# Attention scores computed twice, keys by queries the second time, in place of transposed probabilities

## The chip, the cores and the metric

The kernel runs on one core of one Trainium2 chip. The metric is the device time of one execution in microseconds (us); of several runs the median counts. The engines of the core are TensorE (PE, with its weight loads shown as PEld), VectorE (DVE), ScalarE (ACT), GpSimd (POOL) and SyncE (SP), which issues the DMAs.

## The reference, cut to what matters

One layer of a hybrid backbone over 2048 latent tokens and 256 context tokens, all in float32. Only the attention is touched by the change:

```python
# 8 query heads share 2 key/value heads (4 to each), head_dim 64
# keys: 256 context + 2048 latent tokens = 2304; queries: 2048 latent tokens
s = jnp.einsum('bqkgd,bnkd->bkgqn', q, keys).astype(jnp.float32) * scale
p = jax.nn.softmax(s, axis=-1)
return jnp.einsum('bkgqn,bnkd->bqkgd', p.astype(vals.dtype), vals)
```

Beside it the layer has a gated linear recurrence (HGRN2) in four heads and two directions, an input projection ahead of both, an output projection behind them, and a SwiGLU feed-forward block.

## The kernel before, in words

The stages follow one another: modulation vectors, input projection (with the normalisation and rotation of queries and keys running beside it, `qk_side`, L426), attention together with the recurrence (L566 to L975), output projection (`project_token`, L1005), feed-forward (L1114 to L1264). Matrix products take float32 values as a high part and a low part in a faster type (fp32r): product = high by high, high by low, low by high.

For scores, high and low are packed along the 128 rows of the contraction. `s_k` holds for each key 64 rows of high parts and 64 of low ones; `s_q` holds for each query its high part twice (rows 0 to 63 and 64 to 127), and also its low part twice. Two products into the same PSUM bank give the score. `qk_side` writes `s_q` with four DMAs per 128 tokens and key/value head (L478 to L481), in rows of 2 KB.

The attention is a loop over 64 items (L900): 2 key/value heads, 16 blocks of 128 queries, 2 pairs of heads. An item (`class Pair`, L788) does for each of its two heads, in three segments of 768 keys:

- `scores` (L798): four products with 128 queries as the stationary operand and 512 or 256 keys moving (L812) into one of two PSUM buffers; DVE takes the extremum of the segment (L815; the queries carry a factor -1/8, so a minimum serves as the maximum); ACT computes the exponential with that extremum as bias and sums its rows on the side (L820). For the last segment the extremum of all three is used (L819), and POOL then multiplies the first two segments by a factor (L823, L827).
- `transposes` (L830): the probabilities have queries in the partitions, but the product with V needs keys there. So 36 blocks of 128x128 are transposed by PE (L835), four to a PSUM bank, and copied back to SBUF by ACT, or for two of nine by DVE (L839, L841).
- `products` (L843): 18 products with V as the stationary operand, 64 columns wide, alternating between the lower and the upper 64 partitions of the output (L848). The profile records each float32 product as two.
- `finish` (L860): two transposes back, division by the row sums on DVE (L865 to L870), a sum of the two halves on POOL (L872), a store.

The order of PE's work is written out by hand (`manual_schedule`, L899): PE runs the attention's instructions in the order of the program text. The order on the other engines comes from the tile framework's planner, and each engine's queue is then first in, first out. While item n's scores are computed, item n-1's transposes stand between the segments, and n-1's products come at its end. `other()` (L887) advances the recurrence by 0.88 of a step after five of the six segments. The recurrence has some 276 steps, each a few products on PE (L624 to L727) with element-wise work on POOL (L618 to L661), DVE (L638, L666, L689, L712) and ACT between; two of its units are in progress at a time, and they share one PSUM buffer (`ps_h`).

Of the kernel before, what the change touches and what calls it, by code (L numbers as in the profile page):

```python
# [16 lines left out]
P = 128  # L17
D = 1024
# [25 lines left out]
N_S, N_T, N_H = 2, 2, 1  # L44
LIVE = 2
EV_DVE = (2, 5)
QI = WOE = "gpsimd"
SLOTS, STEPS = 5, 4.4
# [19 lines left out]
def block_kernel(ctx: ExitStack, tc: tile.TileContext, a: dict, out: bass.AP, dbg=None):  # L68
# [21 lines left out]
    s_q = [dram(f"s_q{j}", [NCH, P, 2, 512]) for j in range(2)]  # L90
# [117 lines left out]
    with ExitStack() as st:  # L208
# [217 lines left out]
        def qk_side(t, c):  # L426
# [39 lines left out]
            if isq:  # L466
# [11 lines left out]
                for dup in range(2):  # L478
                    for hh in range(2):
                        nc.sync.dma_start(s_q[c][lt, dup * 64:(dup + 1) * 64, hh],  # L480
                                          f32v(sk[hh * 64:(hh + 1) * 64, :]))  # L481
# [84 lines left out]
    with ExitStack() as st:  # L566
        kvp = pool(st, "kvp", 1, side="right")
        qpl = pool(st, "qpl", 2, side="right")
        sm = pool(st, "sma", 8, side="right")
        pp = pool(st, "pp", 4, side="right")  # L570
        op = pool(st, "op", 1, side="right")
        tp = pool(st, "tp", 9, side="right")
        ps_t2 = pool(st, "ps_t2", N_T, PSUM, side="right")
        ps_av = pool(st, "ps_av", 1, PSUM, side="right")
        hst = ExitStack()
        ps_s2 = pool(hst, "ps_s2", N_S, PSUM)
# [8 lines left out]
        for lv in range(7):  # L585
            mf = up.tile([P, P], F32, tag="kt", name=f"mf{lv}", bufs=4)
            nc.sync.dma_start(mf, a["k_mask"][:, lv, :])
            nc.vector.tensor_copy(mask[:, lv, :], mf)
        nrot = [0]
# [194 lines left out]
        SEG = [(o, SW) for o in range(0, NTOK, SW)]  # L784
        NSEG = len(SEG)
        NKT = NTOK // P

        class Pair:  # L788


            def __init__(self, item, kv, qs):
                self.item, self.kv, self.qs = item, kv, qs
                self.nm = "_".join(map(str, item))
                self.ls = sm.tile([P, 2, NSEG], F32, tag="ls", name=f"ls{self.nm}", bufs=5)
                self.fac = sm.tile([P, 2, NSEG - 1], F32, tag="fac", name=f"fac{self.nm}", bufs=5)
                self.prs, self.negs, self.pf = [], [], {}

            def scores(self, hh, i):  # L798

                nm = f"{self.nm}_{hh}"
                if i == 0:
                    self.prs.append(pp.tile([P, NTOK], F32, tag="pr", name=f"pr{nm}"))
                    self.negs.append(sm.tile([P, NSEG + 1], F32, tag="neg", name=f"neg{nm}"))
                pr, neg = self.prs[hh], self.negs[hh]
                k0, n = SEG[i]
                s = ps_s2.tile([P, 1024], F32, tag="s", name=f"s{i}_{nm}")
                for o in range(0, n, 512):
                    w = min(512, n - o)  # L810
                    for half in range(2):
                        nc.tensor.matmul(s[:, o:o + w], self.qs[:, hh, self.item[2], half, :],  # L812
                                         self.kv[0][:, k0 + o:k0 + o + w],
                                         start=(half == 0), stop=(half == 1))
                nc.vector.tensor_reduce(neg[:, i:i + 1], s[:, :n], axis=AX.X, op=ALU.min)  # L815
                m = i
                if i == NSEG - 1:
                    m = NSEG
                    nc.vector.tensor_reduce(neg[:, NSEG:], neg[:, :NSEG], axis=AX.X, op=ALU.min)  # L819
                nc.scalar.activation(pr[:, k0:k0 + n], s[:, :n], AF.Exp, bias=neg[:, m:m + 1],  # L820
                                     scale=-1.0, accum_out=self.ls[:, hh, i:i + 1])
                if i == NSEG - 1:
                    nc.scalar.activation(self.fac[:, hh, :], neg[:, :NSEG - 1], AF.Exp,  # L823
                                         bias=neg[:, NSEG:], scale=-1.0)
                    for j in range(NSEG - 1):
                        pj = pr[:, j * SW:(j + 1) * SW]
                        nc.gpsimd.tensor_tensor(pj, pj, self.fac[:, hh, j:j + 1].to_broadcast([P, SW]),  # L827
                                                op=ALU.mult)

            def transposes(self, k2):  # L830

                pt = ps_t2.tile([P, 512], F32, tag="t", name=f"pt{self.nm}_{k2}")
                for i in range(2):
                    for hh in range(2):
                        nc.tensor.transpose(pt[:, (2 * i + hh) * P:(2 * i + hh + 1) * P],  # L835
                                            self.prs[hh][:, (2 * k2 + i) * P:(2 * k2 + i + 1) * P], ident)
                pf = self.pf[k2] = tp.tile([P, 512], F32, tag="pf", name=f"pf{self.nm}_{k2}")
                if k2 in EV_DVE:
                    nc.vector.tensor_copy(pf, pt)  # L839
                else:  # L840
                    nc.scalar.activation(pf, pt, AF.Copy)  # L841

            def products(self):  # L843

                self.av = ps_av.tile([P, 256], F32, tag="av", name=f"av{self.nm}")
                for n, k2 in enumerate(T_ORDER):
# [7 lines left out]
            def finish(self):  # L854
                finish(*self.item, self.ot, self.ls, self.fac)
# [452 lines left out]
```

## Time and profile before

| | us |
|---|---|
| median of 3 runs | 3580.23 (3574.32 to 3586.11) |
| the profiled execution | 3583.7 |
| its span, first to last instruction | 3581.9 |
| PE busy in the span | 3352.1 |
| POOL busy in the span | 1593.0 |

A line of groups reads: source line, engine, operation, tile written <- tiles read, shapes, count | busy us in total, mean ns of one | idle time of the engine just ahead of them, and what ended it. A line of the timeline reads: start us, duration us, engine, line, operation, tiles, count [idle before <- what ended it]. A line of waits reads: who <- for whom: us in total, times, longest. Matmuls are pipelined, so the pace of a run of them is read from their starts and not from the duration of one.

### The profile page before, as it was taken

The numbers are of one execution on the slowest core, as the hardware profiler recorded it, in microseconds if no ns is written. First come the engines' busy times: TensorE is split into PE (matmuls) and PEld (weight loads), VectorE is DVE, ScalarE is ACT, GpSimd is POOL, SyncE is SP. The second block draws the span as 40 slices with busy tenths as digits, with TensorE's granted clock in tenths as the row PEclk, the third lists the DMA queues.
The fourth block names the chain that finished last, engine by engine and source line by source line (L and its number), as shares of the span: only waits on it lengthen the run. The fifth ranks groups of instructions, "written<-read, shape, count | busy, mean of one in ns | idle before, by whom it ended". The sixth has DMA issues, their size and how long they took to land. (4 is left out here: it accounts for less than half of the span.)

```text
span 3581.9 us, 52481 instructions
## 1 busy us (share of the span) xinstructions
PE 3352.1 (94%) x19588; PEld 2793.6 (78%) x19588; DVE 1757.0 (49%) x3078; ACT 1549.5 (43%) x3167; POOL 1593.0 (44%) x1496
## 2 busy tenths in 40 slices
PE   8999999979999899999999988999999799999997
PEld 5999877968777778777777876888787678887876
DVE  6445555066667677666655474222354332222344
ACT  4322222157767567766654133333433233333232
POOL 4322232068768758768742046555201165553010
PEclk9999999989999999999999999999999899999998
DMA  7244655321121121111005432222445322222553
GB/s 231 95 140 123 176 167 167 109 85 32 36 63 34 33 69 44 31 46 40 23 24 162 159 106 74 91 76 83 150 146 171 121 92 89 73 88 85 162 173 104
DMA packets 315696, 355.97 MB, mean 99 GB/s; under 512 B 27088, under 2 KB 245168, under 8 KB 315184
## 3 DMA queue, kind: packets, MB, share of 16 engines
q1 hardware_dynamic: 315440, 352.61, 31.7%
q8 instruction: 154, 2.52, 0.3%
q14 instruction: 102, 0.84, 0.1%
HBM read 251.85 MB, written 100.68 MB: 98 GB/s over the span
## 5 line engine op out<-in xcount | busy, mean ns | idle before, releaser
L827 POOL TENSOR_TENSOR pr<-pr,fac 128x768 f32<-128x768 f32 x256 | 374.4, 1484 | 215.0 <-DMA mf<-in_k_mask_dram 101.5
L815 DVE TENSOR_REDUCE neg<-s 128x1 f32<-128x768 f32 x384 | 365.1, 954 | 199.0 <-PE s L812 198.4
L812 PE MATMUL s<-K,qs 128*128 128x512 f32 (+1 forms) x1536 | 371.5, 364 | 33.7 <-ACT pr L820 31.6
L820 ACT ACTIVATE pr<-s,neg 128x768 f32<-128x768 f32 x384 | 348.5, 908 | 73.6 <-DVE neg L819 38.1
L812 PEld LDWEIGHTS s<-K,qs 128*128 128x128 f32 x1536 | 264.0, 191 | 104.8 <-ACT pr L820 44.9
L835 PE MATMUL pt<-identr,pr 128*128 128x128 f32 x2304 | 319.8, 274 | 7.6 <-DVE oo L870 3.2
L841 ACT ACTIVATE pf<-pt 128x512 f32<-128x512 f32 x448 | 256.7, 601 | 111.4 <-PE pt L835 109.5
L1230 PE MATMUL pd<-dl,hh 128*128 128x512 f32 x704 | 277.8, 395 | 2.7 <-DVE dl L1226 2.7
L1230 PE MATMUL pd<-dh,hl 128*128 128x512 f32 x704 | 277.4, 394 | 0.0
L835 PEld LDWEIGHTS pt<-identr,pr 128*128 128x128 f32 x2304 | 261.3, 141 | 16.6 <-ACT pf L841 7.5
L848 PE MATMUL av<-pf,V 128*64 128x256 f32 x2304 | 268.7, 388 | 1.5 <-DVE pf L839 1.5
L848 PEld LDWEIGHTS av<-pf,V 128*64 128x64 f32 x2304 | 162.4, 139 | 88.3 <-issue 9.7
L1230 PE MATMUL pd<-dh,hh 128*128 128x512 f32 x704 | 181.7, 394 | 17.9 <-DVE yy L1244 14.4
L1245 POOL TENSOR_TENSOR yy<-yy,xf 128x512 f32<-128x512 f32 x24 | 30.6, 1296 | 364.6 <-DVE yy L1244 348.7
L1221 ACT ACTIVATE hh<-hr 128x512 fp32r<-128x512 f32 x88 | 55.4, 630 | 292.2 <-PE pd L1230 289.4
L1222 DVE TENSOR_TENSOR hl<-hr,hh 128x512 fp32r<-128x512 f32 x88 | 61.7, 701 | 231.7 <-ACT hh L1221 229.8
L1230 PEld LDWEIGHTS pd<-dh,hh 128*128 128x128 f32 x704 | 133.6, 190 | 48.8 <-DVE yy L1244 16.2
L635 PE MATMUL pa<-Q,M 128*128 128x128 f32 x896 | 131.4, 291 | 30.7 <-POOL Q L661 16.8
L1230 PEld LDWEIGHTS pd<-dl,hh 128*128 128x128 f32 x704 | 134.3, 191 | 31.7 <-DVE dl L1226 3.6
L1230 PEld LDWEIGHTS pd<-dh,hl 128*128 128x128 f32 x704 | 134.3, 191 | 28.2
L635 PEld LDWEIGHTS pa<-Q,M 128*128 128x128 f32 x896 | 116.4, 195 | 38.7 <-POOL Q L661 20.5
L1161 PE MATMUL pA<-x,A11h 128*128 128x512 f32 x352 | 118.9, 403 | 23.9 <-ACT A11h L1135 23.9
(290 smaller groups left out, 8698.8 us busy)
## 6 DMA issues: line engine op xcount, KB each, us to landing
w<-in_w_gu_dram SPq DMA_DIRECT2D x88, 512.0 KB
wr<-in_w_down_dram SPq DMA_DIRECT2D x88, 512.0 KB
wm<-in_w_mod_dram SPq DMA_DIRECT2D x24, 1024.0 KB
s_hid<-h SPq DMA_DIRECT2D x88, 256.0 KB
hr<-s_hid SPq DMA_DIRECT2D x88, 256.0 KB
s_q<-sq SPq DMA_DIRECT2D x128, 128.0 KB
qs<-s_q SPq DMA_DIRECT2D x32, 512.0 KB
ws<-in_w_in_dram SPq DMA_DIRECT2D x9, 1024.0 KB
```

What stands on the lines that cost most here:

```text
L635: nc.tensor.matmul(pa[:, cs], M[:, cs], strided(Q[:], c * P, [[2 * hs, 64 // hs], [512 + hs, 2], [1, hs]]), start=True, stop=True)
L812: nc.tensor.matmul(s[:, o:o + w], self.qs[:, hh, self.item[2], half, :], self.kv[0][:, k0 + o:k0 + o + w], start=(half == 0), stop=(half = ...
L815: nc.vector.tensor_reduce(neg[:, i:i + 1], s[:, :n], axis=AX.X, op=ALU.min)
L820: nc.scalar.activation(pr[:, k0:k0 + n], s[:, :n], AF.Exp, bias=neg[:, m:m + 1], scale=-1.0, accum_out=self.ls[:, hh, i:i + 1])
L827: nc.gpsimd.tensor_tensor(pj, pj, self.fac[:, hh, j:j + 1].to_broadcast([P, SW]), op=ALU.mult)
L835: nc.tensor.transpose(pt[:, (2 * i + hh) * P:(2 * i + hh + 1) * P], self.prs[hh][:, (2 * k2 + i) * P:(2 * k2 + i + 1) * P], ident)
L841: nc.scalar.activation(pf, pt, AF.Copy)
L848: nc.tensor.matmul(self.av[i * 64:(i + 1) * 64], self.kv[1][:, 2 * k2 + i, :], self.pf[k2][:, i * 256:(i + 1) * 256], start=(n == 0), stop ...
L1161: nc.tensor.matmul(acc, w[wi][:, k, :], x[xi][k], start=(start and k == 0 and i == 0), stop=(stop and k == KH - 1 and i == 2), skip_group_ ...
L1221: nc.scalar.activation(hh, hr, AF.Copy)
L1222: nc.vector.tensor_tensor(hl, hr, f32v(hh), op=ALU.subtract)
L1230: nc.tensor.matmul(acc[j][hf], l[:, j * P:(j + 1) * P], r[:, hf * 512:(hf + 1) * 512], start=(ff == 0 and i == 0), stop=(ff == NFF - 1 and ...
```

## The change

Scores are computed twice. The first time is as before, queries by keys, only to find the maximum of each query over all 2304 keys. The second time it is keys by queries (128 keys stationary, 4 heads x 128 queries = 512 columns moving), so that the result already has keys in the partitions. The maximum is subtracted inside the product: a second copy of the keys' high parts (`K2`) has -1 in rows 0 and 1, zeros up to row 63 and the high parts in rows 64 to 127; the low parts of the queries (`ql`) carry the maxima, split into high and low, in rows 0 and 1. ACT then takes the exponential without a bias, and its output goes into the product with V as it is. Row sums are made by adding the 18 tiles of a unit: 7 of the 18 form a chain on DVE and 11 a chain on POOL (the first tile of a chain needs no add), POOL adds the two chains, and four products with a column of ones sum over the partitions.

The unit of work is now 4 heads x 128 queries, 32 units in all. While unit n goes through its 18 tiles of keys (`exps`), the 12 segments of the first score pass of unit n+1 (`maximum`) stand between them. At the end the maxima of n+1 are transposed into two rows (`maxima_in_rows`), and then come the products of n with V. `other` advances the recurrence by 0.47 of a step 19 times per unit. Queries are stored as high parts twice (`s_qh`) and low parts once (`s_ql`), by six DMAs in rows of 512 bytes instead of four in rows of 2 KB. Cut to its core:

```diff
-N_S, N_T, N_H = 2, 2, 1
+N_H = 1
-EV_DVE = (2, 5)
-SLOTS, STEPS = 5, 4.4
+STEP, STEP0 = 0.47, 0.5
+ADD_DVE = (1, 3)
+AT = {1 + 3 * i // 2: (i,) for i in range(12)}
...
-                for dup in range(2):
-                    for hh in range(2):
-                        nc.sync.dma_start(s_q[c][lt, dup * 64:(dup + 1) * 64, hh],
-                                          f32v(sk[hh * 64:(hh + 1) * 64, :]))
+                parts = f32v(sk).rearrange("p (r a t) -> p r a t", r=2, a=2)
+                for hh in range(2):
+                    rows = slice(hh * 64, (hh + 1) * 64)
+                    for dup in range(2):
+                        nc.sync.dma_start(s_qh[c][lt, dup * 64:(dup + 1) * 64, :, hh], parts[rows, :, 0])
+                    nc.sync.dma_start(s_ql[c][lt, :, :, hh], parts[rows, :, 1])
...
+        ps_s1 = pool(hst, "ps_s1", 2, PSUM)
+        ps_s2 = pool(hst, "ps_s2", 2, PSUM)
...
+        K2 = [kvp.tile([P, SW], F32R, name=f"K2_{j}") for j in range(NKB)]
+        QL = [qpl.tile([P, 512], F32R, name=f"ql{j}", bufs=1) for j in range(2)]
+        for t in K2:
+            nc.vector.tensor_copy(t[:64], zero.to_broadcast([64, SW]))
+            nc.vector.tensor_copy(t[:2], less.to_broadcast([2, SW]))
...
+        class Unit:
+            def __init__(self, n):
...
+                nc.sync.dma_start(f32v(self.qh), s_qh[self.g][self.qt].rearrange("p r h t -> p (r h t)"))
+                nc.sync.dma_start(f32v(self.ql[64:]), s_ql[self.g][self.qt].rearrange("p r h t -> p (r h t)"))
+                nc.sync.dma_start(f32v(self.ql[:2]), zrow)
...
+            def maximum(self, i):
...
+                j, b = divmod(i, 4)
+                s = ps_s1.tile([P, 1024], F32, tag="s", name=f"s{self.n}_{i}")
+                for o in range(0, SW, 512):
+                    w = min(512, SW - o)
+                    for half, (q, k) in enumerate(zip((self.qh, self.ql), self.keys(j))):
+                        nc.tensor.matmul(s[:, o:o + w], q[:, b * P:(b + 1) * P], k[:, o:o + w],
+                                         start=(half == 0), stop=(half == 1))
+                nc.vector.tensor_reduce(self.mx[:, b, j:j + 1], s[:, :SW], axis=AX.X, op=ALU.min)
+                if i == 4 * NSEG - 1:
+                    neg = sm.tile([P, 4], F32, tag="neg", name=f"neg{self.n}")
+                    nc.vector.tensor_reduce(neg, self.mx, axis=AX.X, op=ALU.min)
+                    self.mt = sm.tile([P, 4, 2], F32R, tag="mt", name=f"mt{self.n}")
+                    nc.scalar.activation(self.mt[:, :, 0], neg, AF.Copy)
+                    nc.vector.tensor_tensor(self.mt[:, :, 1], neg, f32v(self.mt[:, :, 0]), op=ALU.subtract)
+
+            def maxima_in_rows(self):
+                pm = ps_h.tile([P, 512], F32R, tag="h", name=f"pm{self.n}")
+                for b in range(4):
+                    nc.tensor.transpose(pm[:2, b * P:(b + 1) * P], self.mt[:, b, :], identr)
+                nc.scalar.activation(self.ql[:2], f32v(pm[:2]), AF.Copy)
+
+            def exps(self, t):
+                j, o = t // TSEG, t % TSEG * P
+                s = ps_s2.tile([P, 512], F32, tag="s2", name=f"z{self.n}_{t}")
+                for half, (q, k) in enumerate(zip((self.qh, self.ql), self.keys(j))):
+                    nc.tensor.matmul(s, k[:, o:o + P], q, start=(half == 0), stop=(half == 1))
+                p = tp.tile([P, 512], F32, tag="pT", name=f"pT{self.n}_{t}")
+                nc.scalar.activation(p, s, AF.Exp, scale=-1.0)
+                self.pT.append(p)
+                a = t % 5 in ADD_DVE
+                eng = nc.vector if a else nc.gpsimd
...
+                    eng.tensor_tensor(x, self.acc[a], p, op=ALU.add)
...
+                if t == NKT - 1:
+                    nc.gpsimd.tensor_tensor(self.acc[0], self.acc[0], self.acc[1], op=ALU.add)
+
+            def products(self, V):
+                self.av = ps_av.tile([P, 512], F32, tag="av", name=f"av{self.n}")
+                for t, p in enumerate(self.pT):
+                    i = t % 2
+                    nc.tensor.matmul(self.av[i * 64:(i + 1) * 64], V[:, t, :], p,
+                                     start=(t < 2), stop=(t >= NKT - 2))
...
+            def sums(self):
+                ps = ps_av.tile([P, 512], F32, tag="av", name=f"sum{self.n}")
+                for b in range(4):
+                    nc.tensor.matmul(ps[:, b:b + 1], self.acc[0][:, b * P:(b + 1) * P], ones,
+                                     start=True, stop=True)
...
+        for n in range(NU):
...
+            for t in range(NKT):
...
+                cur.exps(t)
+                if nxt is not None:
+                    for i in AT.get(t, ()):
+                        nxt.maximum(i)
+                if old is not None:
+                    if t == 2:
+                        old.sums()
+                    if t == 4:
+                        old.finish()
...
+                other(STEP)
+            if n + 2 < NU:
+                units[n + 2] = Unit(n + 2)
+            other(STEP)
+            if nxt is not None:
+                nxt.maxima_in_rows()
...
+            cur.products(V)
```

More of the change, by code (lines that the diff above doesn't have):

```diff
@@ L783, in block_kernel @@
         SW = 768
[L784 to L785 removed]
+        NSEG = NTOK // SW
         NKT = NTOK // P
[L788 to L802, printed above, removed]
[L803 to L855 removed]
@@ L876, in load_kv @@
[L876 to L883 removed]
+        TSEG = SW // P
+        NKB = NSEG + 1
+        zero = op.tile([64, 1], F32, name="zero")
```

220 lines of the change are left out of this document (111 added, 109 removed).

## The prediction

> **What bounds the kernel now.** First the page's busy line and, from the busy times by stretch, the row of the attention stage (columns: PE, PEld, DVE, ACT, POOL busy, clock, DMA share, GB/s).
>
> ```profile
> PE 3352.1 (94%) x19588; PEld 2793.6 (78%) x19588; DVE 1757.0 (49%) x3078; ACT 1549.5 (43%) x3167; POOL 1593.0 (44%) x1496
> 729.40:1911.00 1181.60, 1073.21 (x8072) 892.07 (x8072) 799.86 (x1358) 803.82 (x1827) 851.47 (x907) 0.98 0.16 48
> ```
>
> TensorE (PE) is busy 94% of the span, and 91% of the attention stage, where POOL (72%), ACT and DVE (68% each) are loaded too and DMA (16%) is not. The change lies in this stage, so I read its PE timeline next: its ends, and one item whole.
>
> ```profile
> 729.46 1.65 PE L812 MATMUL s<-K,qs 128*128 128x512 f32 x8
> ...
> 772.79 4.11 PE L848 MATMUL av<-pf,V 128*64 128x256 f32 x36
> ...
> 1003.05 4.11 PE L848 MATMUL av<-pf,V 128*64 128x256 f32 x36
> 1007.09 0.97 PE L812 MATMUL s<-K,qs 128*128 128x512 f32 x4
> 1007.90 1.04 PE L835 MATMUL pt<-identr,pr 128*128 128x128 f32 x8
> 1008.69 0.95 PE L812 MATMUL s<-K,qs 128*128 128x512 f32 x4
> ...
> 1019.71 4.11 PE L848 MATMUL av<-pf,V 128*64 128x256 f32 x36
> ...
> 1882.81 4.11 PE L848 MATMUL av<-pf,V 128*64 128x256 f32 x36
> ...
> 1925.09 4.11 PE L848 MATMUL av<-pf,V 128*64 128x256 f32 x36
> ```
>
> The L848 groups stand at the end of each of the 64 items; two come after 1882.81, so 61 items lie between 772.79 and 1882.81: 18.2 us each, **36.4 us for a pair**, which is one unit of the changed kernel. Within an item PE hardly rests: products 4.04 us (1003.05 to 1007.09), a segment of scores 0.81, eight transposes 0.79. The last L848 ends at 1925.09 + 4.04 = 1929.1, but output-projection products run among the last items:
>
> ```profile
> 1900.00:1924.20 24.20, 14.53 (x57) 10.25 (x57) 0.97 0.43 134
> ```
>
> That row is line L1018 alone; without its 14.5 us the stage ends at 1914.6. **The stage is 1914.6 - 729.5 = 1185 us.** What PE and its weight loads wait for in it:
>
> ```profile
> PE pd L624 <- DVE T L666: 12.9, 1, 12.9
> PEld s L812 <- ACT pr L820: 44.9, 51, 8.1
> PEld pa L635 <- POOL Q L661: 20.5, 15, 3.6
> ```
>
> The largest is scores waiting until the exponential (exp) frees their PSUM buffer; the next is the recurrence waiting for POOL.
>
> **The change, per unit of four heads.** What the maximum pass computes is the old score pass: 48 products per unit then and now. Probabilities by V is the same count of columns in half as many instructions. So PE loses the transposes and gains the second scores. For the latter I take the rate of 512-column products of the same type in the output projection, first and last of 47:
>
> ```profile
> 1945.82 0.39 PE L1018 MATMUL y<-wol,mh 128*128 128x512 f32 x1
> 1956.25 0.40 PE L1018 MATMUL y<-woh,ml 128*128 128x512 f32 x1
> ```
>
> 10.43 us over 46 steps is 0.227 us each. Per unit:
>
> - 72 transposes leave: 72 x 0.79 / 8 = **-7.1**.
> - 36 products of 512 columns arrive: 36 x 0.227 = **+8.2**.
> - Row sums by a column of ones: 4 products, which f32 splits into 8 records, at most the 0.11 of a probabilities-by-V record (4.04/36), at least half: I take the upper, **+0.9**. Four transposes that lay the maxima in a row: 0.4.
> - The recurrence's 276 steps issue 1824 records, at that 0.11 an estimated 200 us. They are spread over 30 units instead of 31.5: +0.3 at most, I take 0.2.
>
> PE thus does 2.6 us *more* per unit: a transpose of 128x128 is cheap beside a product of 512 columns.
>
> **The new wait.** PE's order is written out, and `maxima_in_rows` stands right ahead of `products`. The transposes of the maxima need the last maximum, so PE waits for: a reduction over 768 on DVE, the small one, ACT's copy, DVE's subtraction.
>
> ```profile
> L815 DVE TENSOR_REDUCE neg<-s 128x1 f32<-128x768 f32 x384 | 365.1, 954 | 199.0 <-PE s L812 198.4
> L819 DVE TENSOR_REDUCE neg<-neg 128x1 f32<-128x3 f32 x128 | 19.0, 149 | 1.4
> L823 ACT ACTIVATE fac<-neg 128x2 f32<-128x2 f32 x128 | 38.2, 298 | 0.0
> L865 DVE TENSOR_TENSOR ls<-ls,fac x64: 151/168/6258, 762.2 to 1903.2; 128x4 f32<-128x4 f32 x64
> ```
>
> 0.95 + 0.15 + 0.30 + 0.17 = 1.57. Hand-overs and what stands ahead in the two queues have no row: from 0 to 2.2 (one more reduction 0.95, one add 0.68 and one exp 0.60, rows below); I take the half, together 2.7. On average 0.94 recurrence steps of 200 / 276 = 0.7 us stand between: **+2.0** net. Behind the waiting transposes stand all of `products`, so nothing else of PE can use the gap. Bounds: 0.2 (two steps between, empty queues) to 3.8 (no step, full queues).
>
> **What goes.** The wait for the exp (44.9 us over 31 units): -1.4, since only DVE's reduction holds a maximum's buffer now. ACT loses these groups and gets 576 exps of 512 columns at about the 601 ns of L841, so it falls from 804 to at most 804 - 348 - 257 + 576 x 0.60 = 545 us and stops mattering:
>
> ```profile
> L820 ACT ACTIVATE pr<-s,neg 128x768 f32<-128x768 f32 x384 | 348.5, 908 | 73.6 <-DVE neg L819 38.1 <-DVE neg L815 33.6 <-DVE rs_o L737 0.7
> L841 ACT ACTIVATE pf<-pt 128x512 f32<-128x512 f32 x448 | 256.7, 601 | 111.4 <-PE pt L835 109.5
> ```
>
> **POOL and DVE** trade work for work. POOL gives up its rescaling and takes 352 adds of 512; DVE gives up its share of the copies and `ls` and takes 192 adds:
>
> ```profile
> L827 POOL TENSOR_TENSOR pr<-pr,fac 128x768 f32<-128x768 f32 x256 | 374.4, 1484 | 215.0 <-DMA mf<-in_k_mask_dram 101.5 <-ACT fac L823 98.8 <-issue 12.9
> L620 POOL TENSOR_TENSOR Q<-q,F x32: 1277/1299/1753, 744.5 to 1676.4; 128x512 f32<-128x512 f32 x32
> L839 DVE COPY pf<-pt 128x512 f32<-128x512 f32 x128 | 87.0, 680 | 2.7 <-PE pt L835 2.7
> L1092 DVE TENSOR_TENSOR x<-x,x x32: 674/683/1786, 2122.0 to 2614.9; 128x512 f32<-128x512 f32 x32
> ```
>
> POOL: 352 x 1.30 - 374 = +84 us, to 935; DVE: 192 x 0.68 - 87 - 33 = +11. Neither reaches 1185, so I add nothing to the sum; but see the first rival. **The sum per unit:** 36.4 - 7.1 + 8.2 + 0.9 + 0.4 + 0.2 + 2.0 - 1.4 = **39.6 us**.
>
> **Ends.** Start: twelve maxima at DVE's 0.954 (11.4), the recurrence's first wait (12.9, above), the new wait 2.7: 27. Last unit, without maxima: 18 exps x 0.60 and products of 8.1 are 19, less 3 in which the output projection fills gaps: 16. Clearing the second key tiles and query tiles takes ten copies on DVE at no more than L839's 0.68, so 0 to 7 us; I take 0, since the last products of the projection run beside it. Stage: 31 x 39.6 + 43 = 1271 us, **+86**.
>
> **DMA and queues.** Queries leave as 192 stores in 512-byte rows instead of 128:
>
> ```profile
> 350.00:650.00 300.00, 291.11 (x1686) 249.29 (x1685) 161.38 (x420) 77.68 (x159) 80.72 (x61) 0.99 0.57 166
> L480 SPq DMA_DIRECT2D s_q<-sq x128: 445/588/1942, 358.3 to 647.0; - x128
> ```
>
> 64 more issues at 0.588 are 38 us on SP, spread over 290 us in which PE is 97% busy: 0, or up to 20 if that cover fails. Loads of a unit's queries wait for the last product of two units before and have products (8.1) and the new wait to land: 0, or some us per unit if SP stands behind a store.
>
> **Rival 1: DVE and POOL shut each other out.** (3762 us)
>
> ```profile
> 1210.62 9.43 DVE L666 TENSOR_TENSOR T<-F 128x512 f32<-128x512 f32 x1 [0.55 <-POOL Q L661]
> L666 DVE TENSOR_TENSOR T<-F 128x512 f32<-128x512 f32 x16 | 27.2, 1701 | 7.8 <-POOL Q L661 5.0 <-DMA F<-s_f 2.6
> 1215.43 2.89 POOL L827 TENSOR_TENSOR pr<-pr,fac 128x768 f32<-128x768 f32 x2
> 1218.87 0.64 POOL L650 TENSOR_TENSOR C<-M,T 128x256 f32<-128x256 f32 x1
> 1222.61 1.65 PE L812 MATMUL s<-K,qs 128*128 128x512 f32 x4 [7.89 <-ACT pr L820]
> 1225.89 5.52 PE L848 MATMUL av<-pf,V 128*64 128x256 f32 x36
> ```
>
> A DVE product of two SBUF operands, 0.68 alone, took 9.43 and ended as POOL's run did; PE then stood 7.89. The mean of its 16 is 1.70; a 128x4 operation (L865) went from 0.17 to 6.26. The new adds on DVE are of just this kind, 6 per unit: at 1.70 each they cost 6 x 1.02 = 6.1 more, and if half of that reaches PE through late reductions, a unit takes 42.7: +182. It decides once DVE is behind by more than the two score buffers.
>
> The Trainium skill, SBUF — State Buffer, "Who interferes with whom", calls the port that DVE and POOL share an exclusive lock and the only contention among engines. By that rule, splitting the sums over both engines buys little, and this rival is what follows; the 9.43 agrees. The same notes, TensorE: Matmul & The Clock Gate, Part 1, halve PE's clock after an idle window of 3.4 us; the products after the 7.89 took 5.52 instead of 4.11, which agrees; a wait of 2 us would stay below it.
>
> **Rival 2, faster: the smooth unit.** (3545 us) The item at 1003.05 took 16.66, not 18.2. If ACT's relief makes all units like it (-3.1), the wait for exps goes by 0.9 beside that, and recurrence steps cover the new wait down to 0.7, a unit takes 36.4 + 2.6 - 3.1 - 0.9 + 0.7 = 35.7: -35. It decides where a unit falls below (1185 - 43) / 31 = 36.8. For it: ACT at half its load. Against: POOL, which the recurrence waits for, gets busier.
>
> **The numbers.** The profiled execution took 3583.7 (span 3581.9), 3.5 above the median. Forecast 3583.7 + 86 = 3670, less 3.5 and rounded: **3665**, chance 0.52. Rival 1 0.22, rival 2 0.20, and 0.06 for within 0.3%, which is what a measurement of this kernel can tell from no change. Slower 0.74. The range, 3545 to 3790, reaches to rival 2 and past rival 1 (whose adds could reach PE in larger part, as could a wait of 3.8).
>
> **What would show it.** Right: a unit of 38 to 41 us by the V products; PE idle some 2 us ahead of each, released by DVE's subtraction; second scores at 0.23 each. Wrong: PE waiting for maxima's reductions while adds on DVE last over 1.5 us (rival 1), or units below 36.8 with the wait under 1 us (rival 2). A load of queries or a sum on POOL as releaser of PE would be something I cost at nothing.

## The result, and the profile after

The changed kernel takes **3785.4 us** (median of 4 runs, 3777.08 to 3793.14), the kernel before beside it 3578.3: a ratio of 1.0576, with a 95% interval of 1.0546 to 1.0605. So it is slower by 207 us. The forecast was slower by 86.

The page's busy line of the changed kernel, to set against the first line quoted in the prediction:

```profile
PE 3436.1 (91%) x17668; PEld 2729.7 (72%) x17668; DVE 1806.4 (48%) x2896; ACT 1285.6 (34%) x2431; POOL 1723.3 (46%) x1563
```

PE is busy for longer, yet a smaller share of a longer span (3783.1). The busy times by stretch, for the attention up to the last unit but one:

```profile
729.40:2079.60 1350.20, 1134.47 (x6131) 821.89 (x6129) 837.26 (x1155) 524.89 (x1071) 962.57 (x957) 0.93 0.12 37
```

PE's share falls from 91% to 84%, ACT's from 68% to 39%; POOL stays at 71%, where it had 72; the granted clock falls from 0.98 to 0.93. Now PE's timeline: the start, one unit's end, and the V products (L893) of the first and of the 31st unit.

```profile
736.84 0.40 PE L850 MATMUL s<-K,qh 128*128 128x512 f32 x1
755.96 0.77 PE L850 MATMUL s<-K,ql 128*128 128x512 f32 x1 [18.72 <-DMA ql<-s_zero]
...
802.88 9.37 PE L893 MATMUL av<-pT,V 128*64 128x512 f32 x36
...
1224.38 1.07 PE L630 MATMUL pd<-q,kk 128*128 128x128 f32 x8
1228.91 0.52 PE L863 MATMUL pm<-identr,mt 128*2 128x128 f32 x4 [3.46 <-DVE mt L858]
1229.37 9.45 PE L893 MATMUL av<-pT,V 128*64 128x512 f32 x36
...
2079.62 9.29 PE L893 MATMUL av<-pT,V 128*64 128x512 f32 x36
```

From 802.88 to 2079.62 are 30 units: **42.56 us each**, where 39.6 was forecast and 36.28 is the like figure for two items of the kernel before (772.79 to 1861.12). A wait of 18.72 at the start happens once: the load of the row of zeros. It was in no step of the prediction. The two spans differ by 201.2 us: 30 x 6.28 = 188.4 lie in these units, 30.1 ahead of the first V products (802.88 for 772.79), and what is left behind the last of these rows is 17.3 shorter. The loss lies in the attention. What PE waited for in the attention:

```profile
PE pm L863 <- DVE mt L858: 57.7, 22, 4.9
PE pa L641 <- POOL Q L667: 35.6, 17, 5.8
PE s L850 <- DMA ql<-s_zero: 18.7, 1, 18.7
PE pm L863 <- DVE o L748: 15.2, 3, 6.6
PE pa L641 <- DVE S L695: 15.1, 8, 5.2
PE s L850 <- DVE mx L852: 13.7, 16, 3.2
PE po L731 <- DVE o L748: 10.0, 3, 5.7
```

`pm`, the maxima's transposes, leads, as forecast; 57.7 of its 92.8 us are put down to DVE's subtraction (`mt`), the rest to DVE's work for the recurrence. And the recurrence (`pa`, `po`) waits for POOL and DVE more than before, and the reductions (`mx`) have joined. The groups of the new operations:

```profile
L852 DVE TENSOR_REDUCE mx<-s 128x1 f32<-128x768 f32 x384 | 362.1, 949 | 313.7 <-PE s L850 312.2
L883 POOL TENSOR_TENSOR acc<-acc,pT 128x512 f32<-128x512 f32 x288 | 395.7, 1374 | 92.7 <-ACT pT L873 88.6
L883 DVE TENSOR_TENSOR acc<-acc,pT 128x512 f32<-128x512 f32 x160 | 158.0, 988 | 17.7 <-ACT pT L873 16.6
L858 DVE TENSOR_TENSOR mt<-neg,mt 128x4 fp32r<-128x4 f32 x32 | 21.0, 655 | 6.4 <-ACT mt L857 6.4
```

An add takes 1.37 on POOL and 0.99 on DVE, where the prediction had 1.30 and 0.68. To see where a unit's extra time goes I sorted the PE timeline of those 30 units: **idle** is the sum of the waits in brackets, **own** the rest (start to start, slow clock included). Per unit, the kernel before on the left:

| us per unit | before | after | forecast difference | measured |
|---|---|---|---|---|
| first pass (L812, L850) | 9.71 | 8.91 | 0 | -0.80 |
| transposes (L835) | 8.29 | 0 | -7.1 | -8.29 |
| second scores (L871) | 0 | 9.61 | +8.2 | +9.61 |
| V products (L848, L893) | 8.25 | 9.01 | 0 | +0.76 |
| everything else of PE | 7.38 | 8.75 | +1.5 | +1.37 |
| **own** | **33.63** | **36.28** | **+2.6** | **+2.65** |
| idle ahead of `pm` | 0 | 2.91 | +2.0 | +2.91 |
| idle for exps | 0.75 | 0 | -1.4 | -0.75 |
| idle for all else | 1.90 | 3.37 | 0 | +1.47 |
| **idle** | **2.65** | **6.28** | **+0.6** | **+3.63** |

PE's own work came out as forecast, to 0.05 us. The 3 us a unit that were missed are idle time: 0.91 ahead of `pm`, 0.65 of the wait for exps, which had less to give, and 1.47 elsewhere.

### The profile page after: what moved, and what is told of

The parts are those of the page before. It is cut to its first block, busy times and chain, and to the rows that moved or that the text cites. A ratio compares the mean times of both kernels' runs of the same rounds, so it can differ in the third digit from the quotient of the medians.

```text
span 3783.1 us, 48317 instructions
## 1 busy us (share of the span) xinstructions
PE 3436.1 (91%) x17668; PEld 2729.7 (72%) x17668; DVE 1806.4 (48%) x2896; ACT 1285.6 (34%) x2431; POOL 1723.3 (46%) x1563
## 5 line engine op out<-in xcount | busy, mean ns | idle before, releaser
L852 DVE TENSOR_REDUCE mx<-s 128x1 f32<-128x768 f32 x384 | 362.1, 949 | 313.7 <-PE s L850 312.2
L883 POOL TENSOR_TENSOR acc<-acc,pT 128x512 f32<-128x512 f32 x288 | 395.7, 1374 | 92.7 <-ACT pT L873 88.6
L873 ACT ACTIVATE pT<-z 128x512 f32<-128x512 f32 x576 | 332.2, 596 | 197.2 <-PE z L871 193.3
L893 PE MATMUL av<-pT,V 128*64 128x512 f32 x1152 | 289.7, 662 | 0.0
L850 PE MATMUL s<-K,qh 128*128 128x512 f32 (+1 forms) x768 | 267.1, 348 | 17.5 <-DVE mx L852 13.7
L850 PE MATMUL s<-K,ql 128*128 128x512 f32 (+1 forms) x768 | 247.2, 344 | 18.7 <-DMA ql<-s_zero 18.7
L871 PE MATMUL z<-qh,K 128*128 128x512 f32 x576 | 256.5, 445 | 0.3 <-ACT pT L873 0.2
L871 PE MATMUL z<-ql,K 128*128 128x512 f32 x576 | 231.8, 402 | 0.5 <-ACT ql L864 0.5
L893 PEld LDWEIGHTS av<-pT,V 128*64 128x64 f32 x1152 | 88.0, 153 | 179.3 <-issue 177.4
L850 PEld LDWEIGHTS s<-K,qh 128*128 128x128 f32 x768 | 148.7, 194 | 63.5 <-DVE mx L852 25.9
L850 PEld LDWEIGHTS s<-K,ql 128*128 128x128 f32 x768 | 148.4, 193 | 52.4 <-DVE T L672 19.0
L641 PE MATMUL pa<-Q,M 128*128 128x128 f32 x896 | 137.1, 299 | 53.7 <-POOL Q L667 35.6
L883 DVE TENSOR_TENSOR acc<-acc,pT 128x512 f32<-128x512 f32 x160 | 158.0, 988 | 17.7 <-ACT pT L873 16.6
```

The source lines that it names most:

```text
L641: nc.tensor.matmul(pa[:, cs], M[:, cs], strided(Q[:], c * P, [[2 * hs, 64 // hs], [512 + hs, 2], [1, hs]]), start=True, stop=True)
L850: nc.tensor.matmul(s[:, o:o + w], q[:, b * P:(b + 1) * P], k[:, o:o + w], start=(half == 0), stop=(half == 1))
L852: nc.vector.tensor_reduce(self.mx[:, b, j:j + 1], s[:, :SW], axis=AX.X, op=ALU.min)
L871: nc.tensor.matmul(s, k[:, o:o + P], q, start=(half == 0), stop=(half == 1))
L873: nc.scalar.activation(p, s, AF.Exp, scale=-1.0)
L883: eng.tensor_tensor(x, self.acc[a], p, op=ALU.add)
```

## The experiments

Two theories stood at first. **P**: PE's path alone sets the end: its added work, the wait in front of the products, and a clock that falls with the wait. **L**: DVE and POOL, loaded with the adds and shutting each other out, set the pace. The table gives all runs; ratios are to the kernel before on the same chip, the clock is that of 800 to 1800 us, own and idle are taken over 30 units as above. The versions e3, e13, e14 and e15 leave adds out, so their output is not the layer's.

| run | us | ratio (95%) | unit | own | idle | clock |
|---|---|---|---|---|---|---|
| before | 3578.3 | 1 | 36.28 | 33.63 | 2.65 | 0.99 |
| after | 3785.4 | 1.0576 (1.0546 to 1.0605) | 42.56 | 36.28 | 6.28 | 0.94 |
| e1_after_products | 3691.3 | 1.0297 (1.0280 to 1.0314) | 39.45 | 35.34 | 4.11 | 0.96 |
| e2_warm | 3778.0 | 1.0540 (1.0520 to 1.0561) | 42.27 | 38.07 | 4.20 | 0.97 |
| e3_few_adds | 3634.9 | 1.0137 (1.0108 to 1.0166) | 37.96 | 34.83 | 3.13 | 0.97 |
| e4_half_first_pass | 3764.6 | 1.0502 (1.0482 to 1.0521) | 42.00 | 33.72 | 8.28 | 0.89 |
| e5_adds_on_pool | 3772.8 | 1.0575 (1.0549 to 1.0601) | 42.32 | 36.20 | 6.13 | 0.93 |
| e6_adds_on_dve | 3842.2 | 1.0773 (1.0751 to 1.0795) | 44.96 | 37.43 | 7.53 | 0.91 |
| e7_ones_column | 3831.5 | 1.0743 (1.0722 to 1.0765) | 43.98 | 41.15 | 2.83 | 0.97 |
| e8_ones_after_products | 3759.5 | 1.0546 (1.0519 to 1.0573) | 41.58 | 40.27 | 1.31 | 1.00 |
| e9_half_pass_early_maxima | 3650.0 | 1.0218 (1.0192 to 1.0245) | 38.67 | 32.68 | 5.99 | 0.93 |
| e10_lagged_adds | 3772.7 | 1.0563 (1.0531 to 1.0595) | 42.42 | 36.23 | 6.19 | 0.94 |
| e11_lag_early_maxima_steps | 3658.8 | 1.0244 (1.0217 to 1.0272) | 39.11 | 35.81 | 3.30 | 0.97 |
| e12_all_half_pass | 3618.1 | 1.0129 (1.0101 to 1.0157) | 37.50 | 32.60 | 4.90 | 0.94 |
| e13_no_dve_adds | 3715.7 | 1.0376 (1.0334 to 1.0418) | 40.53 | 35.95 | 4.58 | 0.93 |
| e14_no_pool_adds | 3697.2 | 1.0326 (1.0291 to 1.0360) | 39.91 | 35.67 | 4.24 | 0.95 |
| e15_all_few_adds | 3478.3 | 0.9709 (0.9679 to 0.9738) | 32.90 | 31.04 | 1.86 | 0.99 |
| e16_sums_on_pe | 3607.8 | 1.0123 (1.0102 to 1.0144) | 37.00 | 35.43 | 1.57 | 0.99 |

### e1: the maxima's transposes behind the products

```diff
-                nxt.maxima_in_rows()
...
             cur.products(V)
+            if nxt is not None:
+                nxt.maxima_in_rows()
```

> The transposes of the maxima are moved behind the products with V, so PE has about 8 us of products to run while DVE and ACT prepare the maxima. Theory P (PE's path: the added PE work, the wait ahead of the products and the slow clock behind it made the stage longer): the 93 us of waits ahead of these transposes fall to about 30 us (ACT's copy of the maxima is now exposed ahead of the first exponential), the products of a unit go from 9.0 to 7.9 us; 3690 us, between 3670 and 3720. Theory L (DVE and POOL, which shut each other out, set the pace): their work is the same, so PE waits for them elsewhere; above 3750 us.

It took 3691.3, as P expected and well below L's 3750: the place of the wait costs 94 us. PE's timeline and its waits in this run:

```profile
1035.95 7.95 PE L893 MATMUL av<-pT,V 128*64 128x512 f32 x36
1043.83 0.40 PE L863 MATMUL pm<-identr,mt 128*2 128x128 f32 x4
```

```profile
PE pa L641 <- POOL Q L667: 36.9, 18, 5.8
PE z L871 <- ACT ql L864: 24.4, 32, 3.7
```

The products take 7.95, where 9.45 stood behind the wait of 3.46: moving the wait also takes the slow stretch behind it away. But the wait for POOL's Q stays at 36.9, and a new one, for ACT's copy of the maxima, takes 24.4.

### e2: useless products in the wait

```diff
+            def warm(self, V):    # the first 6 of the 18 products, computed ahead of the wait as well
...
+            cur.warm(V)
             if nxt is not None:
                 nxt.maxima_in_rows()
```

> PE computes 6 of the 18 products with V a first time (results overwritten) in the place where it waits for the maxima, so the wait is filled with about 2.6 us of PE work. If idle time slows PE's clock for what follows (theory P with the clock): products of a unit at 7.9 us instead of 9.0, clock of the stage above 0.93, 3745 to 3775 us although PE does 80 us more. If the clock has no part in it: products stay at 9 us, and the filling outlasts some of the waits: 3795 to 3805 us. Theory L: within 10 us of 3785.

3778.0. PE does six products a unit for nothing (2.6 us), and the unit is no longer: idle falls by 2.1, and the real products take 8.25 instead of 9.01. The stretch from 800 to 1800 us, after and here (the granted clock is the third number from the end):

```profile
800.00:1800.00 1000.00, 850.80 (x4584) 607.63 (x4584) 618.47 (x854) 392.15 (x803) 718.72 (x712) 0.94 0.12 34
800.00:1800.00 1000.00, 897.66 (x4877) 619.86 (x4876) 624.26 (x855) 391.90 (x802) 721.10 (x713) 0.97 0.12 34
```

So PE's rest does slow the products behind the wait, as P's clock part says. But the time itself lies 3 us above the band for that, and within the 10 us of 3785 that L gave; as a remedy the filling is worth 7 us at most, which the intervals of the two ratios do not tell from nothing.

### e3: few adds

```diff
-                    eng.tensor_tensor(x, self.acc[a], p, op=ALU.add)
-                    self.acc[a] = x
+                        eng.tensor_tensor(x, self.acc[a], p, op=ALU.add)   # only an engine's first add of a unit
+                        self.acc[a] = x
```

> Of the adds of the row sums only the first on DVE, the first on POOL and the sum of the two are left (15 of 18 per unit gone), so the output is divided by a partial sum. Theory L: DVE and POOL set the pace, so with 158 us less on DVE and 396 us less on POOL the time falls by 150 us or more, below 3640 us. Theory P: only the queues ahead of the last reduction and the recurrence's waits for POOL get shorter: 40 to 70 us less, 3715 to 3745 us.

Of the 17 adds of a unit (the joining one counted) 14 are gone; the text above says 15 of 18. 3634.9: **150 us less**, and P misses. The same rows in this run:

```profile
PE pm L863 <- DVE mt L858: 46.3, 25, 3.5
PE pa L641 <- POOL Q L667: 14.6, 10, 3.0
```

The wait ahead of `pm` shrinks a little, that for Q by 21 us; `pa` waits 2.8 for `S` instead of 15.1, `s` 2.5 for `mx` instead of 13.7, and `po` 1.5 for `o` instead of 10.0. No PE instruction was removed, and yet PE's own time fell by 1.45 us a unit: the clock rose from 0.94 to 0.97.

### e4: half of the first pass

```diff
-                    for half, (q, k) in enumerate(zip((self.qh, self.ql), self.keys(j))):
-                        nc.tensor.matmul(s[:, o:o + w], q[:, b * P:(b + 1) * P], k[:, o:o + w],
-                                         start=(half == 0), stop=(half == 1))
+                    nc.tensor.matmul(s[:, o:o + w], self.qh[:, b * P:(b + 1) * P], self.keys(j)[0][:, o:o + w],
+                                     start=True, stop=True)
```

> The first score pass uses the high parts of the queries alone: 24 products fewer per unit, all else as it was (the maximum subtracted is then that of slightly rounded scores, which cancels in the softmax). Theory P: PE's path, so 24 products (12 of 512 and 12 of 256 columns, 4.1 us per unit) come off one for one: 130 us less, 3640 to 3680 us. Theory L: PE has slack, at most 40 us less, above 3745 us.

3764.6, only 21 us less, where P expected over 100. The waits and the stretch from 800 to 1800 us:

```profile
PE pm L862 <- DVE mt L857: 56.8, 20, 5.7
PE pa L641 <- POOL Q L667: 51.7, 23, 6.2
PE po L731 <- DVE o L748: 21.7, 6, 5.3
```

```profile
800.00:1800.00 1000.00, 797.01 (x4071) 539.73 (x4068) 611.38 (x862) 399.58 (x814) 728.61 (x723) 0.89 0.12 34
```

24 products a unit are gone. At full clock they are worth some 4.2 us (half of the 8.51 that the first pass takes in e8); own time fell by only 2.6, because the clock fell to 0.89, and idle rose by 2.0. **PE's work alone is not what sets this kernel's pace.**

### e5 and e6: all adds on one engine

```diff
-ADD_DVE = (1, 3)
+ADD_DVE = ()                    # e5: all on POOL
+ADD_DVE = (0, 1, 2, 3, 4)       # e6: all on DVE
```

L had two readings. **Lock**: DVE's two-operand adds and POOL's work keep each other waiting. **Load**: the amount of work counts.

> All 17 adds of a unit's row sums on POOL, none on DVE (the joining add goes too). The same sums, other engine. Theory Lock (DVE's adds and POOL's work keep each other waiting): DVE has no two-operand add left, so reductions come in time and POOL's adds fall back to 1.26 us: under 3700 us. Theory Load (POOL's amount of work, done in order, makes the recurrence's products late for PE): POOL gains 6 x 1.27 x 32 = 244 us of work: over 3800 us, with PE's idle time behind POOL's Q well above 35.6 us.

> All 17 adds of a unit's row sums on DVE, none on POOL. Theory Load: POOL loses 10 x 1.37 x 32 = 438 us, DVE gains 11 x 0.68 x 32 = 239 and stays under the stage: under 3720 us, PE's idle time behind POOL's Q down to some 15 us as in the run with few adds. Theory Lock: 17 adds now meet only the recurrence's 12 us a unit on POOL where 6 met 26 us; 17 x 12 is no less than 6 x 26, so no gain: 3760 to 3810 us, with adds on DVE still near 1 us.

All on POOL: a ratio of 1.0575, the same as after, which neither expected. All on DVE: 1.0773, some 70 us slower and above both bands. The adds' group on POOL in e5 and a wait of PE that is new there; then two waits of PE in e6 and its adds on DVE:

```profile
L883 POOL TENSOR_TENSOR acc<-acc,pT 128x512 f32<-128x512 f32 x512 | 660.7, 1290 | 38.2 <-ACT pT L873 18.2
PE sum L899 <- POOL acc L883: 31.6, 9, 8.1
```

```profile
PE pm L863 <- DVE mt L858: 82.8, 22, 8.1
PE pa L641 <- POOL Q L667: 15.3, 8, 3.9
L883 DVE TENSOR_TENSOR acc<-acc,pT 128x512 f32<-128x512 f32 x512 | 413.1, 807 | 20.0 <-ACT pT L873 16.3
```

Without adds on DVE, one on POOL takes 1.29 instead of 1.37, 6% less; but POOL has six more of them, and PE now waits 31.6 us for the last add of the sums, where it had waited 2. With all adds on DVE, PE's wait for Q falls to 15.3, as Load expected, and an add on DVE to 0.81, against Lock; but the adds now stand in the queue of the maxima's reductions, and the wait at the unit's end grows from 57.7 to 82.8. So Load's reading, that POOL alone counts, falls too: in both runs PE loses at one engine what it gains at the other, or more.

### e7 and e8: row sums from a column of ones

```diff
-            V = kvp.tile([P, NKT, 64], F32, tag="V", name=f"V{g}")
+            V = kvp.tile([P, NKT, 65], F32, tag="V", name=f"V{g}")
+            nc.gpsimd.memset(V[:, :, 64:65], 1.0)
...
-                    nc.tensor.matmul(self.av[i * 64:(i + 1) * 64], V[:, t, :], p,
-                                     start=(t < 2), stop=(t >= NKT - 2))
+                    nc.tensor.matmul(self.av[:65], V[:, t, :], p,
+                                     start=(t == 0), stop=(t == NKT - 1))
```

> A 65th column of ones in V makes the products give the row sums: all 17 adds, the joining add, the sums' own products and the last add of two halves go; 18 products of 65 columns into one accumulator instead of two of 64. Nothing of the computation is left out. Theory that the adds are what was mis-sized: as with 15 of 18 adds left out or less, 3590 to 3640 us. Theory that PE's path sets the end: only the sums' 0.8 us a unit go, 3750 to 3765 us.

> The 65th column, and the maxima's transposes moved behind the products. Theory that the wait at a unit's end and the adds are two prices: 94 us below the run with the 65th column alone, 3500 to 3560 us. Theory that they are one (the adds make the chain late, and the chain is where PE meets it): within 30 us of that run.

e7 is slower than after (1.0743), against both expectations; e8 is 72 us below e7, nearer to two prices than to one, and in neither band. The reason is in the timeline of e8, one unit's products, and in its stretch from 800 to 1800 us:

```profile
1161.36 15.61 PE L881 MATMUL av<-pT,V 128*65 128x512 f32 x36
1176.41 0.81 PE L864 MATMUL pm<-identr,mt 128*2 128x128 f32 x4
```

```profile
800.00:1800.00 1000.00, 967.03 (x4491) 636.51 (x4490) 466.27 (x729) 398.36 (x824) 350.27 (x452) 1.00 0.12 35
```

From start to start, 18 products of 65 columns take 15.05, as against 7.88 for 18 of 64 in alternating halves (e1's rows). I read this as the two halves having run side by side; no run has 64 columns in one half throughout. The adds' gain is there (idle 1.31, the least of all runs, clock 1.00), but the products eat it. Here PE is the bound.

### e9 to e12: mending the wait, the queue and the first pass

e9 puts the maxima's transposes inside the products (after 14 of 18), halves the first pass and drops the row of zeros. For e10, a new theory **Queue**: after a unit's last add POOL stands until PE has read the sums, behind the products, and the recurrence's work stands behind POOL's next add. So each add is issued four tiles later:

```diff
                 cur.exps(t)
+                if t >= LAG:
+                    cur.add(t - LAG)
+                elif old is not None:
+                    old.add(NKT - LAG + t)
```

e11 joins the lag, the early transposes and recurrence steps between the products; e12 adds to it e9's half pass without zeros.

> Three edits: the maxima's transposes stand inside the products (after 14 of 18), so neither the chain ahead of them nor ACT's copy behind them stops PE; the first pass takes only the high parts of the queries (24 products fewer a unit; the maximum taken off is then that of the rounded scores, which the division by the sum takes out again); the row of zeros and its load go. From the run with the transposes behind the products (3691): less 24 for ACT's copy and 19 for the load gives 3648. Theory Queue (POOL, with its adds and what stands behind them, sets the pace once the chain is away): the 24 products are again worth nothing, 3620 to 3660 us. Theory PE: they are worth 31 x 4.2 = 130, 3510 to 3540 us.

> Only the adds are issued later: the add of a key tile four tiles after its exp, the last four and the joining add in the first tiles of the next unit, the sums at tile 5 instead of 2. Same work on the same engines. Theory Queue (POOL's first add of a unit waits for the sums, which stand behind the products on PE, and the recurrence's work stands behind that add): the adds fill the time of the products, POOL's 206 us of waiting for the sums fall under 60, PE's idle time behind POOL's Q under 20 us: 3670 to 3725 us. Theory Load (the amount of work on POOL, wherever it stands): 3765 to 3800 us.

> The lagged adds, the maxima's transposes inside the products, and a recurrence step after every fourth product (0.39 steps a place instead of 0.47, so as many a unit). Nothing of the computation is changed. Theory Queue: the prices add up, 3785 - 94 (chain) - 24 (ACT's copy) - 60 to 110 (queue) = 3560 to 3610 us, level with the kernel before, PE idle under 2.5 us a unit and its clock at 0.98 or over. Theory Load: 3650 to 3690 us.

> The run before this one, with the first pass from the high parts of the queries alone and without the row of zeros. Theory Queue: PE is the bound by then, so the 24 products that had been worth 21 us are worth 31 x 4.2 = 130 now, and the load 19: 3420 to 3480 us. Theory Load (POOL at 31 us of work a unit and what it waits for): no gain from the 24 products, 3620 us or more.

e9 (1.0218) lies in Queue's band and not in that of theory PE. e10 is level with after (1.0563), in Load's band. POOL's wait for the sums, after and in e10:

```profile
POOL acc L883 <- PE sum L901: 211.5, 23, 15.8
POOL acc L888 <- PE sum L906: 94.4, 16, 20.0
```

That stand shrank by half, though not under 60 as expected, and PE's wait for Q fell from 35.6 to 28.3, not under 20; the time did not move. e11 (1.0244) lies in Load's band and e12 (1.0129) 2 us below it, both above what Queue expected. So three runs of four are against **Queue**. From e11 to e12 PE's own time falls by 3.2 and idle rises by 1.6: half of the removed work is again given back.

### e13 to e15: which adds

```diff
+                    if t < 5 or not a:      # e13: 5 of DVE's 6 adds left out; e14: "or a", 8 of POOL's 10; e15: e12 with both
                         eng.tensor_tensor(x, self.acc[a], p, op=ALU.add)
                         self.acc[a] = x
```

> Left out: 5 of the 6 adds of a unit on DVE (1.0 is added to the sums, so that none is near zero); POOL's 10 stay. Theory that DVE's two-operand adds are the price (they hold up the maxima's chain and lock POOL out): most of the 150 us, under 3680. Theory that POOL's amount is: within 40 of the changed kernel, 3745 us or more. Theory that both engines bind together: 3690 to 3740.

> Left out: 8 of the 10 adds of a unit on POOL; DVE's 6 stay. Theory that DVE's adds are the price: 3745 us or more. Theory that POOL's amount is: under 3680. Both together: 3690 to 3740.

> The run with all edits and the half first pass, with 13 of its 16 adds of a unit left out. Theory that the amount of adds is what still holds it: PE becomes the bound; its own work was 36.3 us a unit in the changed kernel, less 4.2 (half pass), less some 1.5 (clock back at full), so 31 x 30.6 + idle of 1.3 a unit: 3440 to 3500 us. Theory that the adds' price was the chain's (gone here already): 3590 us or more.

Against after's 1.0576, DVE's adds are worth 0.0200 (some 72 us) and POOL's 0.0250 (89); together 0.0450, and e3, with both away, had 0.0439. So the prices of the two engines **add up**, within intervals of some 0.004 for each ratio; neither alone is the bound. Both lie in the band expected of the two engines together. In e15 the adds are worth 0.0420 (1.0129 less 0.9709), 150 us, even with the wait at the unit's end mended, and it lies in the band that the theory of their amount gave:

```profile
800.00:1800.00 1000.00, 943.36 (x5213) 648.34 (x5212) 623.32 (x966) 507.02 (x1017) 560.63 (x660) 0.99 0.16 46
```

PE is busy 94% there at a clock of 0.99, and a unit takes 32.9.

### e16: the sums on PE, in four groups of columns

```diff
+                for t, p in enumerate(self.pT):
+                    i = t % 4
+                    nc.tensor.matmul(su[i * 32:(i + 1) * 32], ones32, p,
+                                     start=(t < 4), stop=(t >= NKT - 4))
```

> The run with all edits and the half first pass, with every add of the row sums taken from POOL and DVE: 18 products a unit of 32 columns of ones, in four groups of columns in turn, add the key tiles up in PSUM, behind the products by V. Nothing is left out. If four groups run side by side as two halves do (18 products of 65 columns took 15.05 us, in halves of 64 they take 8.0), a unit pays a quarter of 15.05, 3.8 us: 3478 + 31 x 3.8 less the three adds kept there = 3575 to 3605 us. If they run one after the other: 15 us a unit, over 3850. If in pairs: 7.5 us, 3690 to 3720.

It took 3607.8, just above what was expected for four groups side by side. One unit's sums on PE's timeline:

```profile
793.53 4.49 PE L887 MATMUL su<-pT,ones 128*32 128x512 f32 x36
797.95 0.50 PE L868 MATMUL z<-qh,K 128*128 128x512 f32 x1
```

18 products in 4.42 from start to start, where the 65 columns took 15.05. This version computes everything and is the best found, level with e12; it stays 1.2% above the kernel before. No run that computes everything beats that kernel.

## Why the prediction was wrong

The sign was right, and the time lies in the range, at its edge; the forecast itself was 120 us short. By its own steps:

- **PE's work (+2.6 a unit): right as a sum, by errors that cancel.** The transposes gave back 8.29 rather than 7.1; the second scores cost 9.61 rather than 8.2 (9.38 even at a clock of 1.00 in e8: 0.26 a product, and not the 0.227 of the output projection; there one behind another score product takes 0.233, one behind a product of the recurrence 0.31 to 0.33); the first pass got 0.80 shorter. The slow clock is in the sum, too: the same products take 1.45 a unit less in e3, at 0.97 for 0.94. That it came out to 0.05 us is luck. (The recurrence has 1840 records in the stage and not 1824, which moves no term.)
- **The wait ahead of the products: right in place, right in releaser for 57.7 of 92.8 us, too small in size.** 2.91 a unit rather than 2.0. The sum of the chain's parts was fair at a quiet unit's end, but DVE's queue there is not quiet:

```profile
1222.58 0.94 DVE L852 TENSOR_REDUCE mx<-s 128x1 f32<-128x768 f32 x1
1223.45 1.12 DVE L672 TENSOR_TENSOR T<-T 128x8 f32<-128x8 f32 x1
1224.49 0.94 DVE L852 TENSOR_REDUCE mx<-s 128x1 f32<-128x768 f32 x1
1225.36 1.65 DVE L883 TENSOR_TENSOR acc<-acc,pT 128x512 f32<-128x512 f32 x1
1226.93 0.94 DVE L852 TENSOR_REDUCE mx<-s 128x1 f32<-128x768 f32 x1
1227.91 0.17 DVE L855 TENSOR_REDUCE neg<-mx 128x4 f32<-128x12 f32 x1
1228.35 0.42 DVE L858 TENSOR_TENSOR mt<-neg,mt 128x4 fp32r<-128x4 f32 x1 [0.27 <-ACT mt L857]
```

  An add of 1.65 and a product of 1.12 stand between the last three reductions. PE had its last score behind it at 1224.38 (L630 above), 2.55 us before the last reduction began. A second cause was in no term. The transposes write into `ps_h`, the one buffer that they share with the recurrence, and must wait until DVE has read the recurrence's last product out of it:

```profile
1363.83 1.23 DVE L858 TENSOR_TENSOR mt<-neg,mt 128x4 fp32r<-128x4 f32 x1
1368.20 0.69 DVE L748 TENSOR_TENSOR o<-po,rs_o 128x512 f32<-128x512 f32 x1
1369.04 0.58 PE L863 MATMUL pm<-identr,mt 128*2 128x128 f32 x4 [6.64 <-DVE o L748]
```

  Here the maxima were ready at 1365.06, and PE stood another 4 us. In eight of the 31 units they were ready 0.8 to 7.1 us before the transposes; PE's rest beyond that point is some 15 us, 0.5 a unit.
- **"A wait of 2 us would stay below it": the mean does not tell.** The waits of single units run from 0.9 to 6.6. Of the 31 units of the changed kernel, all 13 with a wait of 3.4 or more took 9.06 to 10.62 for the products (1228.91 and 1229.37 above are one); of the 18 below that, 11 took 7.95 and 7 took 9.26 to 10.02. One of the quick ones:

```profile
1448.38 0.40 PE L863 MATMUL pm<-identr,mt 128*2 128x128 f32 x4 [2.19 <-DVE mt L858]
1448.71 7.95 PE L893 MATMUL av<-pT,V 128*64 128x512 f32 x36
```

  The Trainium skill, TensorE: Matmul & The Clock Gate, Part 1, has the clock halve after an idle window of some 3.4 us. The 13 rows agree, and so do three of the 7 others, where PE had rested 4.5 to 5.8 for the recurrence less than 8 us earlier; for the other four it does not account. The prediction applied that rule to an average. The slowing is worth about 1 us a unit: 9.01 for the products after, 8.00 in e1.
- **"Neither reaches 1185, so I add nothing to the sum": the step that failed.** The adds cost some 150 us (e3), more than the 120 that the forecast was short, though POOL is busy 71% of the stage, no more than before, and DVE 62%. POOL and DVE need not be full to hold PE up: PE's order is written out, so each time that a result of theirs is late, PE stands, with all that is queued behind. With the adds in the queues, PE's idle time for the recurrence and the reductions rose from 1.90 to 3.37 a unit; without them, in e3, it is 1.07. And PE's rest lowers the clock, which accounts for another 1.45 a unit between after and e3.
- **The start: another wait than the one counted.** Of each unit's query loads, that of the row of zeros was passed over; the first one ended 18.7 us after PE was ready. The prediction had named a load of queries as something that it costs at nothing. But the recurrence's first wait, which it put at 12.9, is not on PE's timeline there, so the start is some 6 us off by these two. Where the row of zeros is left out, PE waits at the start for POOL instead, 15.05 in e9.
- **Rival 1 came within 23 us, by a mechanism that was not the main one.** It forecast a unit of 42.7 from DVE adds of 1.70. They took 0.99, and with none on DVE (e5) the time is the same. The Trainium skill, SBUF — State Buffer, "Who interferes with whom", calls the port that the two engines share an exclusive lock. The prediction inferred that splitting the sums over both buys little, and e5 agrees (1.0575 and 1.0576). The engines do lengthen each other's adds: one takes 0.83 on DVE when most of POOL's are away (e14), and 1.30 on POOL when most of DVE's are (e13). For 5 adds a unit on DVE and 9 on POOL that makes 1.5 us of engine time. But e6 speaks against it as the main cause: with every add on DVE one takes 0.81, and the kernel is slower.
- **The wait for exps (-1.4)** was there, but only 0.75 of it was on PE's own timeline; the 44.9 that the prediction took was the row of the weight loads.

What stays open: how the 1.47 of added idle time divides between POOL's and DVE's lateness. The experiments show that the prices add up, not which wait each pays. Also why four units with waits of 0.9 to 3.0 us and no long wait close ahead have slow products.

## What to carry to other kernels

Ask what a layout gave for nothing. With keys along the free axis, ACT summed the rows of its exponentials on the side; with keys in the partitions the same sums cost 17 adds a unit (14 of them 4.6 us, between after and e3), or 4.5 us of PE (e16). With the second scores' 9.6 that is more than the 8.3 that the transposes had cost. And where one engine runs in a written order, work on the engines that feed it is not free below 100%: look at which results it waits for, and price what is queued ahead of them. To find out what a removed piece of work is worth, remove it and look at idle time and clock together: e4 removed 4.2 us a unit and got 0.6.

## What the runs showed of the hardware

- **The granted clock follows PE's idle time, run by run**: 1.3 to 2.7 us of idle a unit goes with 0.99 to 1.00, 2.8 to 3.3 with 0.97, 4.1 to 4.9 with 0.93 to 0.97, 6.0 to 6.3 with 0.93 or 0.94, 7.5 with 0.91, 8.3 with 0.89. So a wait is paid twice, and PE work taken away behind a wait comes back as a slower clock. e2, which fills the wait, is the test of cause: 0.94 to 0.97.
- **Products that take turns at different groups of output columns took less time, as if side by side**: from start to start, 18 of 64 columns in two halves take 7.88 us, 18 of 65 columns in one group 15.05, 18 of 32 columns in four groups 4.42. The Trainium skill, TensorEngine Tiling (Array Packing), "Overview", gives up to 2 times and 4 times for such tiles; against the 65 columns, 1.91 and 3.40 are measured.
